# Tuning numbers of a fused decoder block: fewer expert rows on POOL during the key search, more on DVE ahead of the gate spreading, and every eighth instead of every fourth V tile multiplied in plain fp32

## The chip, the core and the metric

The kernel runs on one core of one Trainium2 chip. The metric is device time of one execution in microseconds; before the change three runs gave 1669.54, 1673.44 and 1673.93 us, median 1673.44.

The engines are called as in the profile: PE (matrix multiplication, with PEld for its weight loads), DVE (vector engine), ACT (scalar engine), POOL (GpSimd, which also issues the indirect gathers) and SP (which issues most plain DMAs). Each engine works through its own instructions in a fixed order and waits on semaphores.

## The reference, cut to what matters

One decoder layer on 512 tokens of width 1024: RMSNorm, one input projection, three attention branches, a gated merge, and then a product-key expert layer. All inputs and outputs are fp32. The first half is not touched by the change. The expert layer is:

```python
def peer_ffn(h, w_q, keys1, keys2, u, v):
    q = (h @ w_q).reshape(B, S, PEER_HEADS, 2, half)           # 8 heads
    s1 = einsum('bshd,hkd->bshk', q[..., 0, :], keys1)         # 128 keys each
    s2 = einsum('bshd,hkd->bshk', q[..., 1, :], keys2)
    v1, i1 = top_k(s1, 16); v2, i2 = top_k(s2, 16)
    cand = v1[..., :, None] + v2[..., None, :]
    sv, si = top_k(cand.reshape(..., 256), 16)
    experts = i1[si // 16] * 128 + i2[si % 16]                 # 128 experts per token
    gates = softmax(sv)
    act = gelu(h . u[experts]) * gates
    return sum(act * v[experts])                               # u, v: 16384 x 1024
```

So every token picks 128 of 16384 experts, and needs one row of `u` and one row of `v` for each.

## The kernel before, in words

The 512 tokens are four blocks of 128. The kernel computes the expert layer in two different ways. Blocks 0 and 1 are **gathered**: for each of the 128 choices of a token, POOL issues an indirect DMA that brings one row of `peer_u` or `peer_v` for every one of the 128 tokens (a tile of 128 x 1024 fp32, 512 KB), and an engine consumes it. Such a tile is called a *row* in this document; there are 2 blocks x 2 tables x 128 = 512 rows. Blocks 2 and 3 are **dense**: all 16384 experts are multiplied with the tokens on PE, 128 experts (one *tile* of 512 KB) at a time, first all of `u` (128 U tiles) and then all of `v` (128 V tiles), with a gate that is zero where a token did not choose the expert.

`step()` handles one row. It first issues the gathers of coming rows (line 810), as far ahead as `ahead` allows (AHEAD = 4, or AHEAD + MORE = 6 once the dense part has begun, where two of seven rows take a buffer of another pool), and then consumes the oldest row. A `u` row is one multiply-and-sum on DVE (line 820). A `v` row is normally one multiply-add on DVE (line 829). With `apart=True` it is instead a multiplication on ACT (line 825) and an addition on POOL (line 826). All row additions of a block go into the same tile (`mg` in the profile), so they follow one another.

The rows are spread over the program by counts:

- 176 rows (EARLY_ROWS) run beside the attention of blocks 1 to 3. They are all 128 `u` rows and the first 48 `v` rows of block 0.
- **The search** (`search`, from line 653 on) finds the top keys for blocks 1 to 3. It is a generator that yields a cost for each piece of DVE work; the loop around it adds these costs to a credit, and whenever the credit reaches PER_ROW it does one `step(apart=True)`. The scheduler of the language places these instructions, at low priority. The search also computes the first 8 U tiles (FIRST_U) between its pieces. Its candidate sums (`cand`, line 668) run on POOL, its copies out of PSUM (`qp`, `s`, lines 695 and 702) on ACT.
- From there on DVE, POOL and PE follow the order in which the code is written (`manual_schedule`); ACT and SP are still ordered by the scheduler. PE computes 24 more U tiles (COVER, line 922). Meanwhile DVE does `weigh` (softmax of the gates) and three times `choose` (the experts' numbers, lines 751 to 781), computes a normalised input (`h2n`, line 793), and then BETWEEN rows with `step()`.
- **The spreading** turns the chosen numbers and gates of the dense blocks into dense gates: 64 rounds of one-hot tiles built on DVE (`o`, line 977), scaled on ACT (line 983), multiplied on PE (line 995), with 25 more U tiles and 0.7 rows per round in between. PE cannot start the first round until DVE has built the first `o`, and DVE comes to it only after the BETWEEN rows.
- **The V stage** works through the 128 V tiles, with the last 71 U tiles and all rows that are left spread evenly over it. `fetch_v` (line 1026) issues the load of tile k + 3 on SP while tile k is prepared.

A V tile is multiplied in one of two ways. A **split** tile goes into a `raw` buffer (three of them); ACT casts it to fp32r (`whi`, line 1044), DVE forms the rest (`wlo`, line 126), the same is done for the gated activations (`ah` on ACT, `al` on DVE, line 1046), and PE makes 12 matmuls of 128 x 512 (lines 138 to 140). A **plain** tile, every WHOLE-th, goes into a buffer of its own (`last`, one of it), needs neither ACT nor DVE, and PE makes 4 matmuls in fp32 (line 1060), each of which the profile shows as two records. The `raw` buffer of a split tile is free again once both `whi` and `wlo` have been formed from it.

The loop of the V stage, in which one call prepares tile k + 1 before PE is given tile k:

```python
for k in range(NK):
    now, ready = ready, operands(k + 1) if k + 1 < NK else None
    while done[0] < min(len(JOBS), start + (len(JOBS) - start) * (k + 1) // (NK - 5)):
        step()
    while k_u < min(NK, LAG + (NK - LAG) * (k + 1) // (NK - 10)):
        list(dense_u(k_u))
        k_u += 1
    dense_v(k, *now)
```

Of the kernel before, what the change touches and what calls it, by code (L numbers as in the profile page):

```python
# [29 lines left out]
FIRST_U, COVER, DURING, AFTER = 8, 24, 25, 0  # L30
KEPT = FIRST_U + COVER
SPILT = (128 - KEPT) // 2
BETWEEN, UNWEIGHED, IN_RAW = 12, 14, 0
LAG = FIRST_U + COVER + DURING + AFTER
GA_LATE = 6
URING = 6
# [2 lines left out]
GQ_AT, GQ_PARTS = 1, 4  # L39
RAW_MORE = 5  # L40
STEPS_U = 4
WHOLE, STEPS_N = 4, 0.7
AHD = 3
GSPLIT = 4
GT = 4
# [3 lines left out]
AHEAD, ROWS_IN, MORE = 4, 5, 2  # L49
LATER = 400  # L50
PACE = {"search": 9.0, "choose": 8.0, "rows": 3.5}
EARLY_ROWS, PER_ROW = 176, 2.8


@with_exitstack
# [1168 lines left out]
```

## Time and profile before

The profiled execution took 1678.19 us, of which the span from its first to its last instruction is 1676.2 us; the median of the runs is 1673.44 us, 4.75 us below the profiled one.

| | PE | PEld | DVE | ACT | POOL |
|---|---|---|---|---|---|
| busy, us | 1587.3 | 1371.1 | 1361.5 | 721.4 | 853.2 |
| share of the span | 95% | 82% | 81% | 43% | 51% |

DMA moved 531.79 MB, 317 GB/s on the mean. The mean granted PE clock was 0.977.

How to read it: the profile shows for each instruction its engine, its line in the kernel, its start and its duration, and for the idle time before it the event that ended that idle time. PE's records overlap, since matmuls are pipelined; so the cost of a group of matmuls is read from the start of its first one to the start of the next group, not from the sum of durations. A wait that the profile shows on an engine costs something only if that engine, or one that waits for it, is the one that ends last in that stage.

### The profile page before, as it was taken

To read this page: it belongs to the slowest core of one execution; us is meant where nothing else is said; L and a number is where in the kernel's file an instruction comes from. 1 tells how busy PE (TensorE), PEld (TensorE's weight loads), DVE (VectorE), ACT (ScalarE), POOL (GpSimd) and SP (SyncE) were. 2 spreads that over 40 slices of the span, in tenths; PEclk is the share of its full clock that TensorE was granted. 3 is DMA by queue.
4 is the path that set the end of the run, shared out by engine and by line. 5 is a ranking of instruction groups with operands and counts; after the bars stand their busy time and mean duration, and the time that the engine had idled before them with its cause. 6 is when DMAs were issued, how large, how long until landed. Compare 5 with 4: busy or idle time off the path is not lost.

```text
span 1676.2 us, 25413 instructions
## 1 busy us (share of the span) xinstructions
PE 1587.3 (95%) x8718; PEld 1371.1 (82%) x8718; DVE 1361.5 (81%) x2625; ACT 721.4 (43%) x1586; POOL 853.2 (51%) x664
## 2 busy tenths in 40 slices
PE   6999789999998988998998999999999999999998
PEld 6999679898887988987887999677777777777775
DVE  4777678788988999997998998677777787877886
ACT  6887567546445434543415765222222222222221
POOL 0200251766566455778935544455545555655552
PEclk8999999998998999999999999999999999999999
DMA  6787464898898899767878999999999999999995
GB/s 263 240 262 231 127 199 146 305 354 300 298 344 288 297 338 352 276 212 248 280 247 323 339 354 351 396 405 395 356 389 400 402 397 402 389 401 402 402 368 215
DMA packets 209841, 531.79 MB, mean 317 GB/s; under 512 B 18224, under 2 KB 88112, under 8 KB 209712
## 3 DMA queue, kind: packets, MB, share of 16 engines
q0 software_dynamic: 73728, 268.47, 43.4%
q1 hardware_dynamic: 131376, 249.12, 42.1%
q10 hardware_dynamic: 4608, 12.58, 1.9%
q8 instruction: 69, 1.13, 0.3%
q14 instruction: 60, 0.49, 0.1%
HBM read 515.42 MB, written 14.68 MB: 316 GB/s over the span
## 4 chain that ended last, share of the span: by engine, by line
PE 34%; issue 20%; DMA 20%; POOL 11%; DVE 11%; ACT 2%; SPq 0%; POOLq 0%; DVEq 0%; ACTq 0%
PE mm L922 10%; POOL row L810 9%; DMA row<-in_peer_u_dram,eidx 9%; DMA row<-in_peer_v_dram,eidx 8%; PE mm L139 5%; PE mm L140 5%; PE mm L138 5%; DVE wlo L126 3%; DVE mg L829 2%; DVE scr L820 2%; PE sc L995 2%; PE tp L995 2%; ACT whi L114 1%; POOL mg L826 1%; DMA raw<-in_w_pq_dram 1%
## 5 line engine op out<-in xcount | busy, mean ns | idle before, releaser
L810 POOL DMA_INDIRECT row<-in_peer_u_dram,eidx x256 | 327.0, 1277 | 247.6 <-DVE scr L820 169.4
L810 POOL DMA_INDIRECT row<-in_peer_v_dram,eidx x256 | 331.2, 1294 | 238.1 <-DVE mg L829 170.3
L126 DVE TENSOR_TENSOR wlo<-raw,whi 128x1024 fp32r<-128x1024 f32 (+1 forms) x259 | 327.2, 1265 | 70.0 <-ACT whi L114 41.8
L820 DVE SCALAR_TENSOR_TENSOR scr<-row,h2n 128x1024 bf16<-128x1024 f32 x256 | 313.4, 1224 | 44.3 <-DMA row<-in_peer_u_dram,eidx 42.0
L829 DVE SCALAR_TENSOR_TENSOR mg<-row,acts,mg 128x1024 f32<-128x1024 f32 x222 | 284.7, 1282 | 34.0 <-DMA row<-in_peer_v_dram,eidx 30.7
L114 ACT CAST whi<-raw 128x1024 fp32r<-128x1024 f32 (+1 forms) x172 | 180.5, 1051 | 129.4 <-PE mm L139 59.9
L922 PE MATMUL mm<-h2f,hhi 128*128 128x256 f32 x960 | 220.7, 381 | 2.9 <-ACT ga L924 2.9
L922 PE MATMUL mm<-h2f,hlo 128*128 128x256 f32 x960 | 219.2, 379 | 0.0
L922 PEld LDWEIGHTS mm<-h2f,hlo 128*128 128x128 f32 x960 | 180.5, 190 | 31.9 <-issue 7.2
L922 PEld LDWEIGHTS mm<-h2f,hhi 128*128 128x128 f32 x960 | 180.3, 191 | 27.6 <-ACT ga L924 3.3
L138 PE MATMUL mm<-whi,hhi 128*128 128x256 f32 (+1 forms) x576 | 166.9, 292 | 7.1 <-DVE g L551 1.9
L139 PE MATMUL mm<-wlo,hhi 128*128 128x256 f32 (+1 forms) x576 | 166.1, 289 | 1.0 <-DVE wlo L126 1.0
L140 PE MATMUL mm<-whi,hlo 128*128 128x256 f32 (+1 forms) x576 | 164.3, 287 | 2.4 <-DVE hlo L610 1.6
L924 ACT ACTIVATE ga<-mm 128x256 f32<-128x256 f32 x116 | 44.3, 383 | 279.8 <-PE mm L922 272.1
L1044 ACT CAST whi<-raw 128x1024 fp32r<-128x1024 f32 x96 | 100.3, 1046 | 107.8 <-DMA raw<-in_peer_v_dram 105.7
L138 PE MATMUL mm<-hhi,whi 128*128 128x384 f32 x320 | 111.4, 348 | 7.3 <-ACT ga L924 4.3
L138 PEld LDWEIGHTS mm<-whi,hhi 128*128 128x128 f32 x576 | 109.6, 191 | 10.6 <-ACT hhi L604 2.3
L186 POOL TENSOR_TENSOR rsy<-rsv,mhalf 128x4 f32<-128x4 f32 (+5 forms) x25 | 42.0, 1683 | 145.3 <-DVE rsv L185 144.4
L140 PEld LDWEIGHTS mm<-whi,hlo 128*128 128x128 f32 x576 | 109.8, 191 | 4.5 <-DVE hlo L610 2.0
L139 PEld LDWEIGHTS mm<-wlo,hhi 128*128 128x128 f32 x576 | 110.0, 191 | 3.7 <-DVE wlo L126 1.7
L139 PE MATMUL mm<-hlo,whi 128*128 128x384 f32 x320 | 111.2, 348 | 0.0
L140 PE MATMUL mm<-hhi,wlo 128*128 128x384 f32 x320 | 110.6, 346 | 0.0
(274 smaller groups left out, 3276.4 us busy)
## 6 DMA issues: line engine op xcount, KB each, us to landing
raw<-in_peer_v_dram SPq DMA_DIRECT2D x96, 512.0 KB
hlo<-in_uT_dram SPq DMA_DIRECT2D x60, 512.0 KB
hhi<-in_uT_dram SPq DMA_DIRECT2D x60, 512.0 KB
raw<-in_w_nat_dram SPq DMA_DIRECT2D x40, 512.0 KB
last<-in_peer_v_dram SPq DMA_DIRECT2D x32, 512.0 KB
raw<-in_w_tr_dram SPq DMA_DIRECT2D x48, 256.0 KB
raw<-in_w_o_dram SPq DMA_DIRECT2D x24, 512.0 KB
raw<-in_w_tr_dram SPq DMA_DIRECT2D x24, 512.0 KB
```

Of the source, the lines that this page charges most:

```text
L114: A.copy(hi[:, :n * w], raw[:, :n * w])
L126: V.tensor_sub(lo, raw, hi.bitcast(F32))
L138: PE.matmul(ps, lh, rh, start=first, stop=False)
L139: PE.matmul(ps, lh, rl, start=False, stop=False)
L140: PE.matmul(ps, ll, rh, start=False, stop=last)
L810: G.indirect_dma_start(out=r, out_offset=None, in_=t["peer_" + tab], in_offset=bass.IndirectOffsetOnAxis(ap=eidx[b][:, j:j + 1], axis=0))
L820: V.scalar_tensor_tensor(scr, r, 1.0, h2n[b], op0=OP.mult, op1=OP.mult, accum_out=acts[b][:, c]))
L829: V.scalar_tensor_tensor(x1[b], r, acts[b][:, c], x1[b], op0=OP.mult, op1=OP.add))
L922: PE.matmul(ps[:, :TD], w[:, dc], h2f[dc], start=dc == 0, stop=dc == KC - 1)
L924: A.activation(ga(k), ps[:, :TD], AF.Gelu)
L995: PE.matmul(ps[:, u], o[:, 1, u], o[:, 0, u], start=True, stop=True)
L1044: A.copy(hi, raw)
```

## The change

Three numbers are changed.

```diff
-BETWEEN, UNWEIGHED, IN_RAW = 12, 14, 0
+BETWEEN, UNWEIGHED, IN_RAW = 36, 14, 0
...
-WHOLE, STEPS_N = 4, 0.7
+WHOLE, STEPS_N = 8, 0.7
...
-EARLY_ROWS, PER_ROW = 176, 2.8
+EARLY_ROWS, PER_ROW = 176, 4.6
```

With PER_ROW = 4.6 the search is given 19 rows instead of 34. With BETWEEN = 36 DVE adds 24 more rows ahead of the spreading. The spreading has 44 rows in both, so 237 instead of 246 are left for the V stage. With WHOLE = 8 there are 112 split and 16 plain V tiles, instead of 96 and 32.

On POOL, at the end of the search and after it, the order was this (L826 is an addition of a row, L810 a gather, L668 a candidate sum of the search's last head):

```order
L826 TENSOR_TENSOR mg_2214<-mg_2214,row 128x1024
L668 TENSOR_TENSOR cand<-v_9183 128x3x24
L668 TENSOR_TENSOR cand<-v_9183 128x3x16
L810 DMA row<-in_peer_v_dram,eidx_173 128x1024
L826 TENSOR_TENSOR mg_2214<-mg_2214,row 128x1024
L668 TENSOR_TENSOR cand<-v_9183 128x3x8
L668 TENSOR_TENSOR cand<-v_9183 128x3x16
L810 DMA row<-in_peer_v_dram,eidx_173 128x1024
```

From there gathers and additions alternated until 34 additions were done, and now the same place reads:

```order
L826 TENSOR_TENSOR mg_2214<-mg_2214,row 128x1024
L810 DMA row<-in_peer_v_dram,eidx_173 128x1024
L668 TENSOR_TENSOR cand<-v_9131 128x3x24
L668 TENSOR_TENSOR cand<-v_9131 128x3x16
L668 TENSOR_TENSOR cand<-v_9131 128x3x8
L668 TENSOR_TENSOR cand<-v_9131 128x3x16
L810 DMA row<-in_peer_v_dram,eidx_173 128x1024 x37
```

The first 19 additions stand where they stood, and the 15 that followed, most of them behind the last candidate sum, are gone; on ACT their 15 multiplications (line 825) are gone with them.

On DVE, between the choosing and the first one-hot tile of the spreading (L793 is the normalised input, L829 a row, L977 a one-hot tile, L998 the first product with the gates):

```order
 L793 SCALAR_TENSOR_TENSOR h2n<-mg_7447,rstd,g2r 128x1024
-L829 SCALAR_TENSOR_TENSOR mg_2214<-row,acts_174,mg_2214 128x1024 x12
+L829 SCALAR_TENSOR_TENSOR mg_2214<-row,acts_174,mg_2214 128x1024 x36
 L977 TENSOR_TENSOR o<-tg,eT 128x1024 x4
 L998 TENSOR_TENSOR ga<-sc,ga 128x32x4
```

All four `o` tiles, and so PE's first round, now stand behind 36 rows instead of 12.

On PE, at the fourth V tile, the order was (L922 is a U tile of 8 matmuls, L1060 a plain V tile):

```order
L922 MATMUL mm<-h2f,hhi 128x256 x8
L1060 MATMUL sc<-last,ga 128x512 x2
L1060 MATMUL tp<-last,ga 128x512 x2
L922 MATMUL mm<-h2f,hlo 128x256 x8
L138 MATMUL sc<-whi,ah 128x512
```

and in the place of the plain tile there is now a split one:

```order
L922 MATMUL mm<-h2f,hhi 128x256 x8
L138 MATMUL sc<-whi,ah 128x512
L139 MATMUL sc<-wlo,ah 128x512
L140 MATMUL sc<-whi,al 128x512
L138 MATMUL sc<-whi,ah 128x512
L139 MATMUL sc<-wlo,ah 128x512
```

The U tiles keep their places between the V tiles; 16 of the 32 plain tiles have become twelve matmuls each, with a cast on ACT and two instructions on DVE (lines 126 and 1046) and a `raw` buffer for each.

## The prediction

> **What bounds the kernel now.** The change touches three stretches, so I first asked the table of windows for these: the search of blocks 1 to 3 from its first apart rows to DVE's last instruction of it, the choosing, the rows between, the spreading, the V stage.
>
> ```profile
> 699.50:798.40 98.90, 86.65 (x460) 80.46 (x460) 88.20 (x540) 43.55 (x63) 82.51 (x74) 0.95 0.68 226
> 798.40:869.50 71.10, 68.18 (x317) 59.70 (x316) 66.73 (x94) 21.62 (x35) 46.34 (x27) 1.00 0.78 266
> 869.50:888.60 19.10, 14.72 (x70) 12.72 (x68) 15.33 (x13) 2.35 (x6) 13.59 (x11) 0.97 0.87 319
> 888.60:1039.50 150.90, 149.14 (x931) 138.10 (x932) 142.40 (x186) 103.12 (x350) 71.70 (x60) 0.98 0.94 337
> 1039.50:1672.20 632.70, 624.77 (x2530) 479.16 (x2528) 478.99 (x654) 154.66 (x260) 331.43 (x241) 0.99 1.00 382
> ```
>
> The columns are the stretch and its length, then busy time of PE, PEld, DVE, ACT and POOL, then granted clock, DMA share and GB/s. The V stage is PE's: 624.77 of 632.70 us, with DVE at 479. The spreading is PE's too (149.14 of 150.90). Only from 869.5 to 888.6 does PE have time to spare.
>
> A timeline of PE in the V stage (start, duration, engine, line, operation) says what a tile costs.
>
> ```profile
> 1317.02 1.88 PE L1060 MATMUL sc<-last,late 128*128 128x512 f32 x4
> 1320.45 3.62 PE L922 MATMUL mm<-h2f,hlo 128*128 128x256 f32 x16
> 1323.72 0.58 PE L138 MATMUL sc<-whi,ah 128*128 128x512 f32 x1
> 1326.65 0.40 PE L138 MATMUL sc<-whi,ah 128*128 128x512 f32 x1
> 1329.45 3.62 PE L922 MATMUL mm<-h2f,hlo 128*128 128x256 f32 x16
> 1332.71 0.58 PE L138 MATMUL sc<-whi,ah 128*128 128x512 f32 x1
> ```
>
> From start to start, the plain tile takes 1320.45 - 1317.02 = 3.43 us and the split one that ends at 1329.45 takes 2.80. A U tile takes 3.26, and the split tile behind it, 1323.72 to 1326.65, is longer by 0.13; call it 3.4 together. 96 x 2.80 + 32 x 3.43 + 71 x 3.4 = 620, against the 625 that PE is busy: these prices carry the stage.
>
> **Part 1, every eighth V tile plain.** Sixteen tiles go from 3.43 to 2.80 us on PE: 16 x 0.63 = 10.1 us less. What they add lies on engines that have room only if buffers do. DVE gets 16 forms of `wlo` and `al`, and loses 9 rows:
>
> ```profile
> L126 DVE TENSOR_TENSOR wlo<-raw,whi 128x1024 fp32r<-128x1024 f32 x87 | 106.7, 1226 | 20.8 <-ACT whi L1044 14.7 <-ACT ga L924 4.1 <-issue 2.0
> L1046 DVE TENSOR_TENSOR al<-ga,ah 128x256 fp32r<-128x256 f32 x78 | 32.8, 421 | 53.2 <-ACT ah L1042 53.0
> L829 DVE SCALAR_TENSOR_TENSOR mg<-row,acts,mg 128x1024 f32<-128x1024 f32 x120 | 153.9, 1282 | 25.9 <-DMA row<-in_peer_v_dram,eidx 24.2
> ```
>
> 16 x (1.23 + 0.42) - 9 x 1.28 = +15 us, so 494 of 623 us: 79% busy, from 76%. That is hidden. The 9 rows cost PE nothing and give nothing back.
>
> The buffers are tighter. 96 loads through three `raw` buffers in 633 us left each load 19.8 us; 112 in 623 us leave 16.7. One turn of a buffer, in order of time on SP, ACT, DVE, PE, SP:
>
> ```profile
> 1308.80 0.33 SPq L1026 DMA_DIRECT2D raw<-in_peer_v_dram  x1
> 1317.98 1.05 ACT L1044 CAST whi<-raw 128x1024 fp32r<-128x1024 f32 x1 [0.77 <-DMA raw<-in_peer_v_dram]
> 1327.91 1.22 DVE L126 TENSOR_TENSOR wlo<-raw,whi 128x1024 fp32r<-128x1024 f32 x1
> 1324.84 4.68 SPq L1026 DMA_DIRECT2D raw<-in_peer_v_dram  x2
> ```
>
> The load takes 9.2 us, the cast 1.05, then the data waits 8.9 us for DVE's turn, 1.22 for `wlo`, and the next load (the second of the last row, which ends at 1329.52) goes out at once; PE uses the tile at 1332.71, 3.6 us after `wlo`. So a turn needs 9.2 + 1.05 + 1.22 = 11.5 us and may take 16.7; of the 8.9 us of idling about 3.1 go. That holds on the mean. Where loads are slow it doesn't:
>
> ```profile
> 1409.00 0.37 SPq L1026 DMA_DIRECT2D raw<-in_peer_v_dram  x1
> 1427.48 1.05 ACT L1044 CAST whi<-raw 128x1024 fp32r<-128x1024 f32 x1 [3.30 <-DMA raw<-in_peer_v_dram]
> ```
>
> There 18.5 us passed from issue to cast, a turn of 21. Such stretches, the first tiles, and the last ones, where no U tile gives the loads time, will cost PE something. From below it is nothing (PE has 3.6 us in hand); from above I take one slow turn's excess, 21 - 16.7 = 4.3 us, at three places, 13 us. I take 1.5, near the lower end, since the mean has 5 us of slack a turn. V stage: -10.1 + 1.5 = -8.6 us.
>
> **Part 2, 15 rows fewer on POOL.** The order keeps the first 19 additions where they were, so the search runs as before up to 785. What goes then is a wait. ACT, DVE and PE at the search's end:
>
> ```profile
> 787.14 1.15 ACT L825 ACTIVATE row<-row,acts 128x1024 f32<-128x1024 f32 x1 [7.32 <-DMA row<-in_peer_v_dram,eidx]
> 788.46 0.47 ACT L702 COPY s<-sc 128x384 f32<-128x384 f32 x1
> 788.96 0.68 DVE L657 MAX8 v<-s 128x8 f32<-128x128 f32 x3 [6.79 <-ACT s L702]
> 781.10 0.83 PE L699 MATMUL sc<-keys,qp 128*128 128x128 f32 x6
> 788.61 9.22 PE L922 MATMUL mm<-h2f,raw 128*128 128x256 f32 x32 [3.22 <-ACT ga L924]
> ```
>
> ACT stood 7.32 us before an apart row whose gather had not landed, with the last copy `s` queued behind it, though PE had finished its scores at 781.9; DVE stood 6.79 us for that `s`. This multiplication is one of the 15 that go. `s` can then be copied at 782.0, 6.4 us earlier, and the search ends on DVE at 798.4 - 6.4 = 792.0. PE gains its 3.22, and its U tiles of the cover end near 880.5 instead of 883.7.
>
> The larger effect is in the choosing. DVE's small operations stand still while POOL adds a row:
>
> ```profile
> 802.37 3.63 DVE L736 TENSOR_TENSOR gate<-ex,gden 128x128 f32<-128x128 f32 x3
> 806.08 2.89 DVE L752 TENSOR_SCALAR p<-sh 128x128 f32<-128x128 uint32 x1
> 806.52 2.36 POOL L826 TENSOR_TENSOR mg<-mg,row 128x1024 f32<-128x1024 f32 x1
> 840.73 0.29 DVE L781 TENSOR_TENSOR e<-hot 128x128 f32<-128x128 bf16 x1
> 855.44 0.29 DVE L781 TENSOR_TENSOR e<-hot 128x128 f32<-128x128 bf16 x1
> 855.90 0.23 DVE L752 TENSOR_SCALAR p<-sh 128x128 f32<-128x128 uint32 x1
> 867.51 0.29 DVE L781 TENSOR_TENSOR e<-hot 128x128 f32<-128x128 bf16 x1
> 841.88 2.35 POOL L826 TENSOR_TENSOR mg<-mg,row 128x1024 f32<-128x1024 f32 x1
> ```
>
> The same L752 takes 2.89 us beside an addition (both end at 808.9) and 0.23 after POOL's last one, which began at 841.88. The three choosings end at 840.9, 855.6 and 867.8: 34.9 (from 806.0), 14.7 and 12.2 us. With the 19 additions over by 785 all three take 12.2, which saves 25.2, and the gates ahead of them (the three products of L736 in 3.63 us, which would be near 0.9 at 0.3 each) some 2.7. The stretch of 71.1 us becomes 43, and DVE is ready for rows at 835 instead of 869.5.
>
> **Part 3, 36 rows ahead of the spreading.** This spends what part 2 gave, on the path that sets the end, since PE's first round waits for an `o` that DVE builds behind the rows.
>
> ```profile
> 869.50 10.53 DVE L829 SCALAR_TENSOR_TENSOR mg<-row,acts,mg 128x1024 f32<-128x1024 f32 x8
> 881.25 1.28 DVE L829 SCALAR_TENSOR_TENSOR mg<-row,acts,mg 128x1024 f32<-128x1024 f32 x1 [1.23 <-DMA row<-in_peer_v_dram,eidx]
> 887.40 1.28 DVE L829 SCALAR_TENSOR_TENSOR mg<-row,acts,mg 128x1024 f32<-128x1024 f32 x1 [0.77 <-DMA row<-in_peer_v_dram,eidx]
> 890.36 2.04 PE L995 MATMUL sc<-o 128*128 128x128 f32 x8 [6.14 <-issue]
> 880.00:890.00 10.00, 4.22 (x22) 3.46 (x20) 6.48 (x7) 1.34 (x4) 7.99 (x6) 0.88 1.01 406
> ```
>
> Eight rows that lay ready took 1.32 us each. The next four came 2.05 us apart (881.25 to 887.40 in three steps), held by their gathers, with the DMA at 406 GB/s. From 835: eight rows to 845.6; at 2.05 while PE still draws U tiles, to 880.5, 17 more; the last 11 at 1.32, to 895. The floor is bytes: 29 rows are still to be gathered behind the seven that lie ready, and some 13 U tiles loaded ((880.5 - 835) / 3.4, their six buffers being refilled as they empty), 42 x 0.52 = 22 MB at 406 GB/s, 54 us from 836: 890. I take 893, nearer the paced sum. The spreading starts 893 - 888.6 = 4.4 us later, and PE, done at 880.5, stands 14 us before it. The ends are 882.5 (all 36 at 1.32; then the start is 6 us earlier) and 903 (28 at 2.05; 14 us later).
>
> The Trainium skill (DMA: Bandwidth & Descriptors, section "Where 436 GB/s comes from") puts loads from HBM at about 358 GB/s a core, which speaks against the change: the same bytes would take 61 us, an estimate by that page, the rows would end at 897 and the sum below would be about 4 us worse. The row of 880 to 890 shows 406 GB/s and the V stage 382 over 633 us, so the trace doesn't bear it out, and the sum keeps the measured rate.
>
> The spreading keeps its length; its rounds and its 44 rows are unchanged.
>
> **The sum.** -8.6 + 4.4 = -4.2 us against the profiled 1678.2 us. The profiled execution is 4.8 us above the median of its runs, so I apply the difference to the median: 1673.4 - 4.2 = 1669.2 us. A measurement of this kernel can tell about 0.3%, 5 us, from no change: the three runs shown lie within 4.4.
>
> **The rivals.** First, *the rows keep DVE's pace*. Fewer other loads run from 835 on than I think, or U tiles are fetched well ahead; all 36 rows take 1.32 us, and the spreading starts 6 us earlier, at PE's own end. For it speaks that eight rows in a row did so; against it, the four after them. Sum -8.6 - 6 = -14.6: 1659 us.
>
> Second, *the gathers set the pace throughout*. POOL issues each gather in its own order when a buffer comes free, and these two rows show it at 2.07 us a gather while DVE adds rows:
>
> ```profile
> 885.68 1.77 POOL L810 DMA_INDIRECT row<-in_peer_v_dram,eidx  x1 [0.30 <-issue]
> 887.75 1.76 POOL L810 DMA_INDIRECT row<-in_peer_v_dram,eidx  x1 [0.30 <-issue]
> ```
>
> If that lasts to the end, the spreading starts 14 us later and the sum is -8.6 + 14.4 = +5.8: 1679 us. Against it, 2 us a row is also what a full DMA gives, and its load falls when PE's U tiles are done.
>
> Third, on the slower side too, *the three raw buffers bind in the V stage*. It decides from the point where a turn (load, wait behind SP's other loads, cast, DVE's turn) passes 16.7 us on the mean; then PE waits where it had waited for nothing, and the 10.1 us are given back. At 17.1 us a turn, 112 / 3 x 17.1 = 638 us, the stage is 5.7 us longer than now, and with +4.4 the sum is +10: 1683 us. For it speak the slow loads above; against it, the 8.9 us that a full buffer lay waiting for DVE.
>
> That the change does not do what it says, because the added casts and subtractions on ACT and DVE delay the rows' consumption, falls under the third.
>
> **How the numbers follow.** The forecast, mid stretch 0 to +8 and V stage -10 to -6, a total of -10 to +2, has 0.44: of that 0.16 lies below -5, 0.28 within 5. The first rival has 0.28, all faster. The second has 0.14 and the third 0.14; together 0.02 of them within 5, since they may come in part, and 0.26 slower. So faster 0.44, same 0.30, slower 0.26. The range runs from all gains at once, -10.1 - 6 = -16, 1657 us, to the second rival with the V stage's gain halved, +14.4 - 4.3 = +10, which is also the third: 1684 us; about 0.18 lies outside.
>
> **What would show it.** Right: PE's V stage 8 to 10 us shorter at the same prices a tile, with 16 groups of L1060; DVE's choosing in 43 us with no L752 above 0.3; the search ending near 792; DVE's 36 rows from 835 to about 893 with waits for gathers, and PE idle some 14 us ahead of its first L995. Wrong: waits of PE for `whi` or `wlo` of more than a few us in the V stage, SP waiting for `wlo` ahead of most loads; or rows that end before 885 or after 900.

## The result, and the profile after

The changed kernel takes 1678.85 us (median of 8 runs) against 1669.75 us for the kernel before on the same chip; the ratio is 1.0062, 95% interval [1.0046, 1.0078]. It is slower by 7.7 to 13.0 us; 1669.2 was forecast. The two profiled executions differ by less than the medians, 1682.45 against 1678.19 us, because the one shown of before lay 8.4 us above its median of eight runs and this one 3.6 above. That turns out to matter.

The same stretches in the table of windows of the changed kernel: the search (from its first apart rows), the choosing, the rows up to PE's first product, the spreading, the V stage.

```profile
696.00:788.00 92.00, 79.89 (x438) 75.16 (x436) 87.58 (x540) 38.26 (x58) 73.18 (x68) 0.96 0.67 229
788.00:830.65 42.65, 41.32 (x184) 36.18 (x185) 38.28 (x93) 7.78 (x16) 0.00 (x0) 0.96 0.40 139
830.65:897.42 66.77, 47.19 (x221) 41.32 (x220) 47.91 (x39) 6.34 (x17) 48.80 (x37) 0.88 0.98 389
897.42:1046.74 149.32, 149.32 (x931) 138.19 (x932) 140.29 (x193) 102.58 (x349) 71.89 (x59) 0.99 0.93 333
1046.74:1676.65 629.91, 618.52 (x2594) 491.50 (x2592) 491.88 (x668) 175.87 (x292) 338.20 (x232) 0.99 0.99 377
```

The choosing takes 42.65 us (71.1 before). In the third row PE works 47 of 67 us while the DMA is at 0.98. The V stage is only 2.8 us shorter than the 632.7 before, though PE's busy time in it fell by 6.3. DVE's and ACT's timeline at the search's end and in the choosing:

```profile
778.07 0.48 ACT L702 COPY s<-sc 128x384 f32<-128x384 f32 x1 [0.28 <-issue]
791.97 0.85 DVE L736 TENSOR_TENSOR gate<-ex,gden 128x128 f32<-128x128 f32 x3
792.91 0.23 DVE L752 TENSOR_SCALAR p<-sh 128x128 f32<-128x128 uint32 x1
829.45 1.28 DVE L793 SCALAR_TENSOR_TENSOR h2n<-mg,rstd,g2r 128x1024 f32<-128x1024 f32 x1
830.65 6.56 DVE L829 SCALAR_TENSOR_TENSOR mg<-row,acts,mg 128x1024 f32<-128x1024 f32 x5
838.58 1.28 DVE L829 SCALAR_TENSOR_TENSOR mg<-row,acts,mg 128x1024 f32<-128x1024 f32 x1 [1.38 <-DMA row<-in_peer_v_dram,eidx]
```

The last copy of scores has no apart row ahead of it, the gates' products take 0.85 us (3.63 before) and the first `p` 0.23 (2.89). The rows begin at 830.65. Five of them lie ready; the sixth waits for its gather. How they end, on DVE and PE:

```profile
877.35 0.38 PE L964 MATMUL acc<-cst,e 128*128 128x128 f32 x2
881.45 1.28 DVE L829 SCALAR_TENSOR_TENSOR mg<-row,acts,mg 128x1024 f32<-128x1024 f32 x1 [0.47 <-DMA row<-in_peer_v_dram,eidx]
883.84 11.92 DVE L829 SCALAR_TENSOR_TENSOR mg<-row,acts,mg 128x1024 f32<-128x1024 f32 x9 [1.11 <-DMA row<-in_peer_v_dram,eidx]
895.67 4.61 DVE L977 TENSOR_TENSOR o<-tg,eT 128x1024 f32<-128x1024 f32 x4
897.42 2.04 PE L995 MATMUL sc<-o 128*128 128x128 f32 x8 [19.59 <-issue]
```

PE's work ahead of the spreading ends at 877.8 (its last products start at 877.35); it then stands 19.59 us, until the rest of the rows, the last nine of them in one go, and the first `o` are done. "issue" names no releaser there; the chain is read from DVE's rows and from the order of the code, in which `o` is built on DVE, scaled on ACT and then multiplied on PE. Three windows of that stretch show the DMA full all along, also after PE's last U tile, and PE's clock falling while it idles:

```profile
840.00:850.00 10.00, 10.00 (x48) 8.80 (x47) 5.77 (x5) 0.85 (x3) 7.87 (x7) 1.00 1.02 410
880.00:890.00 10.00, 0.00 (x0) 0.00 (x0) 8.22 (x7) 0.00 (x0) 6.63 (x6) 0.57 1.03 413
890.00:900.00 10.00, 2.58 (x10) 2.52 (x11) 9.86 (x9) 3.08 (x11) 5.08 (x5) 0.50 1.03 413
```

In the V stage the list of waits names PE's (all of them) and the SP queue's (here only those for DVE; SP is the queue that issues the loads of V tiles, line 1026):

```profile
PE sc L138 <- ACT ah L1042: 5.2, 5, 1.6
PE sc L139 <- DVE wlo L126: 2.9, 7, 0.8
PE sc L138 <- ACT whi L1044: 2.8, 2, 1.9
...
SPq L1026 <- DVE al L1046: 136.8, 46, 5.8
SPq L1026 <- DVE wlo L126: 43.3, 16, 4.3
```

PE waits 10.9 us (7.7 before), and 62 waits of SP at its V loads, 180 us in all, end with DVE's `wlo` or `al`, that is, when DVE has just freed a buffer. This is the sign that the third rival (three `raw` buffers bind) would leave. It was one of the first two things to test.

### The profile page after: what moved, and what is told of

Its sections match the earlier page's. It is cut to its first block, busy times and chain, and to the rows that moved or that the text cites. A ratio compares the mean times of both kernels' runs of the same rounds, so it can differ in the third digit from the quotient of the medians.

```text
span 1680.6 us, 25640 instructions
## 1 busy us (share of the span) xinstructions
PE 1578.6 (94%) x8782; PEld 1381.5 (82%) x8782; DVE 1376.6 (82%) x2672; ACT 727.1 (43%) x1603; POOL 837.2 (50%) x649
## 4 chain that ended last, share of the span: by engine, by line
PE 54%; issue 15%; POOL 10%; DMA 10%; DVE 8%; ACT 2%; SPq 0%; POOLq 0%; DVEq 0%; ACTq 0%
PE mm L922 16%; POOL row L810 8%; PE mm L138 7%; PE mm L139 7%; PE mm L140 7%; DMA row<-in_peer_v_dram,eidx 5%; DVE wlo L126 3%; PE sc L995 2%; PE tp L995 2%; DMA raw<-in_peer_v_dram 1%; ACT whi L114 1%; PE sc L140 1%; PE sc L139 1%; PE tp L140 1%; PE tp L138 1%
## 5 line engine op out<-in xcount | busy, mean ns | idle before, releaser
L810 POOL DMA_INDIRECT row<-in_peer_v_dram,eidx x256 | 349.3, 1364 | 264.7 <-DVE mg L829 152.7
L810 POOL DMA_INDIRECT row<-in_peer_u_dram,eidx x256 | 329.4, 1287 | 244.0 <-DVE scr L820 169.0
L126 DVE TENSOR_TENSOR wlo<-raw,whi 128x1024 fp32r<-128x1024 f32 (+1 forms) x275 | 346.1, 1260 | 115.6 <-ACT whi L1044 65.0
L829 DVE SCALAR_TENSOR_TENSOR mg<-row,acts,mg 128x1024 f32<-128x1024 f32 x237 | 303.8, 1282 | 30.3 <-DMA row<-in_peer_v_dram,eidx 27.2
L922 PE MATMUL mm<-h2f,hhi 128*128 128x256 f32 x960 | 220.6, 381 | 0.0
L922 PE MATMUL mm<-h2f,hlo 128*128 128x256 f32 x960 | 219.1, 379 | 0.0
L922 PEld LDWEIGHTS mm<-h2f,hlo 128*128 128x128 f32 x960 | 180.4, 190 | 28.3 <-issue 4.3
L922 PEld LDWEIGHTS mm<-h2f,hhi 128*128 128x128 f32 x960 | 180.4, 191 | 24.5
L1044 ACT CAST whi<-raw 128x1024 fp32r<-128x1024 f32 x112 | 117.0, 1046 | 96.3 <-DMA raw<-in_peer_v_dram 93.0
```

What stands on the lines that cost most here:

```text
L126: V.tensor_sub(lo, raw, hi.bitcast(F32))
L810: G.indirect_dma_start(out=r, out_offset=None, in_=t["peer_" + tab], in_offset=bass.IndirectOffsetOnAxis(ap=eidx[b][:, j:j + 1], axis=0))
L829: V.scalar_tensor_tensor(x1[b], r, acts[b][:, c], x1[b], op0=OP.mult, op1=OP.add))
L922: PE.matmul(ps[:, :TD], w[:, dc], h2f[dc], start=dc == 0, stop=dc == KC - 1)
L1044: A.copy(hi, raw)
```

## The experiments

Three accounts. Theory one: the loss is made ahead of the spreading, behind 36 rows. Theory B (theory two in the first expectations): three buffers eat the V stage's gain. Theory D, formed after the first four runs: the DMA engines are full for nine tenths of the V stage, and a faster PE only waits more often. "First copy of scores" is ACT's first L702 of the three blocks' search; the change touches no code ahead of it, and yet it came anywhere from 670.4 to 681.9 us in these executions. So the middle is measured from it. The length of a V stage is always that of one profiled execution, a time that of the median.

### Only the V tiles

```diff
-WHOLE, STEPS_N = 4, 0.7
+WHOLE, STEPS_N = 8, 0.7
```

> Only WHOLE = 8 (16 plain V tiles instead of 32); search, choosing and the 12 rows as before. Theory one (the loss is made ahead of the spreading, where PE now idles 19.6 us behind 36 rows): the V stage alone still gains, by the 2.8 us that the two profiled executions differ or up to the 8.6 us forecast, so 1661 to 1667 us against a median of 1669.75. Theory two (the three raw buffers take the gain and more, and the loss of about 9 us is made in the V stage): 1672 us or more, with PE waiting for whi, wlo and ah for over 10 us in that stage.

1663.36 us, ratio 0.9982 [0.9962, 1.0001]: about 3 us, at the edge of what can be told. The V stage took 631.27 us, hardly less than before, with PE busy for 618.12. So the V tiles are not where the time was lost, nor do they bring what was forecast. PE waited 12.4 us for `whi`, `wlo` and `ah` in that stage, which is theory two's sign, but no loss came of it. This kernel runs before's program up to the V stage, and here that looks different: PE's first product came at 875.20, 203.7 us behind the first copy of scores at 671.50, with PE idle for 2.86 us. In the execution shown of before it was 890.36 - 679.92 = 210.4 us and 6.14.

### Only the rows

```diff
-BETWEEN, UNWEIGHED, IN_RAW = 12, 14, 0
+BETWEEN, UNWEIGHED, IN_RAW = 36, 14, 0
-EARLY_ROWS, PER_ROW = 176, 2.8
+EARLY_ROWS, PER_ROW = 176, 4.6
```

> Only the rows (PER_ROW = 4.6 and BETWEEN = 36), every fourth V tile plain as before. Theory one: PE's first round of the spreading starts 7 us later than before (897 against 890), after some 20 us of idling, and nothing gives it back: 1676 to 1680 us, V stage within 2 us of its 632.7. Theory two: the middle costs less than 4 us: 1670 to 1674 us.

1680.49 us, ratio 1.0085 [1.0063, 1.0108]. On PE, and on ACT for the first copy of scores:

```profile
674.68 0.50 ACT L702 COPY s<-sc 128x384 f32<-128x384 f32 x1
897.43 2.04 PE L995 MATMUL sc<-o 128*128 128x128 f32 x8 [20.50 <-issue]
```

That is 222.8 us behind the scores, and the V stage took 630.95 us, no longer than before. The whole loss is here; theory one holds.

### The same with 12 and with 24 rows

Both have PER_ROW = 4.6 and every fourth V tile plain; the second has BETWEEN = 24 as well.

```diff
-EARLY_ROWS, PER_ROW = 176, 2.8
+EARLY_ROWS, PER_ROW = 176, 4.6
```

> Only PER_ROW = 4.6, with 12 rows ahead of the spreading as before; the 15 rows that POOL no longer adds all go to the V stage (261 instead of 246). Theory one: rows end near 848, so the first round comes as soon as PE's cover ends, at 878 instead of 890: 1657 to 1660 us if the V stage carries 15 more rows at no cost. Rival (the V stage is held by its DMA, whose share is 1.00 there): 15 more rows of 0.52 MB at 382 GB/s are 20 us more, so 1672 to 1678 us.

> PER_ROW = 4.6 with 24 rows ahead of the spreading, every fourth V tile plain; 249 rows for the V stage (246 before). Seven ready rows from 831 and 17 at 2.05 us end at 875, before PE's cover does at 878. Theory one: the first round starts at 878 to 880, 10 to 12 us earlier than before, V stage as before: 1658 to 1660 us. Rival (the DMA's backlog of U tiles and rows only moves, and the spreading or the V stage gives the time back): 1666 us or more.

With 24 rows PE's first product comes when PE's own cover is done, as theory one says:

```profile
673.01 0.49 ACT L702 COPY s<-sc 128x384 f32<-128x384 f32 x1
870.48 0.38 PE L964 MATMUL acc<-cst,e 128*128 128x128 f32 x2
873.32 1.32 PE L995 MATMUL sc<-o 128*128 128x128 f32 x8 [2.35 <-issue]
```

200.3 us behind the scores, 21 earlier than with 36 rows. But the time is 1668.95 us, ratio 1.0017 [0.9992, 1.0043]; with 12 rows it is 1697.39, ratio 1.0192 [1.0168, 1.0216], although there too PE starts on time (877.06). Their rivals had the direction: the V stage takes back what the middle gives. For 12 rows it takes back far more than the rival's 1672 to 1678 us. Its windows, with 249 and 261 rows left to it:

```profile
1020.68:1656.11 635.43, 625.78 (x2530) 478.95 (x2528) 482.86 (x660) 155.57 (x260) 328.84 (x244) 0.99 1.00 383
```

```profile
1024.42:1691.06 666.64, 635.61 (x2530) 482.11 (x2528) 498.32 (x679) 156.05 (x260) 339.65 (x256) 0.98 0.98 375
```

Most of PE's waits in the second of them come through `ah`, which ACT makes from gates that DVE multiplies in its turn behind the rows:

```profile
PE sc L138 <- ACT ah L1042: 24.0, 13, 5.1
```

PE works on the same tiles as before in both, and yet 15 rows more than before's 246 made the stage 34 to 37 us longer. From this comes theory D, with two windows of the changed kernel, one from the stage's middle and its last 70 us:

```profile
1397.00:1467.00 70.00, 69.98 (x299) 55.96 (x297) 54.99 (x64) 18.39 (x31) 39.63 (x27) 1.00 1.03 393
1607.00:1677.00 70.00, 65.77 (x258) 47.92 (x256) 56.10 (x69) 18.62 (x30) 28.33 (x19) 1.00 0.77 281
```

In stretches of 63 us the DMA's share is 0.95 to 1.04 from the stage's start to some 63 us before its end, and 0.73 in the last; only there is it free.

### Four buffers

```diff
-            pool, n = (gp[0], 1) if k % WHOLE == WHOLE - 1 else (wp, None)
+            pool, n = (gp[0], 1) if k % 4 == 3 else (wp, None)
```

So every fourth tile, split or plain, goes into the buffer `last`. The first run is the changed kernel with this edit, the second the kernel before with WHOLE = 8 and this edit.

> The changed kernel, but every fourth V tile still goes into the buffer of its own (last) that it had before, split or plain; so the split tiles have four buffers as in the kernel before, and PE's order is that of the changed kernel. V stage of the changed kernel 629.9 us. Theory B (three raw buffers take the gain): the stage falls to 622 to 625 us, PE's waits in it from 11 to under 6 us, and the time to 1671 to 1674 us. Theory D (the DMA engines are full for nine tenths of that stage, and PE, made faster, only waits for them more often): stage 628 to 632 us, time 1676 to 1682 us.

> The kernel before with WHOLE = 8 and the same four buffers; rows as before (246 in the V stage). Theory B: V stage 623 to 626 us against 631.3 with three buffers, and 1656 to 1660 us against 1663.4. Theory D: 629 to 633 us in the V stage, 1662 to 1667 us.

The changed kernel with four buffers: 1684.89 us, ratio to before 1.0108 [1.0071, 1.0145], above what either theory expected. The execution profiled was the quickest of its five, 1674.53 us. Its V stage and PE's waits in it:

```profile
1039.52:1668.73 629.21, 614.28 (x2594) 490.31 (x2592) 491.81 (x668) 175.83 (x292) 326.40 (x232) 0.99 0.99 377
```

```profile
PE sc L138 <- ACT ah L1042: 14.3, 7, 5.7
PE sc L139 <- DVE wlo L126: 0.2, 1, 0.2
```

629.21 against 629.91 us, and PE waits 14.5 us instead of 10.9: the waits for `whi` and `wlo` went, those for `ah` grew. The other kernel took 1669.17 us, ratio 1.0019 [1.0002, 1.0036], slower than with three buffers (0.9982), with 637.74 us in the V stage; that too is more than either theory expected. So the fourth buffer does not bring the gain that theory B promised. It does not make SP's waits go either: 151 of the 180 us for `wlo` and `al` are left in the changed kernel. What those waits are worth is shown by the next run, which keeps them. Why the fourth buffer costs time is not shown; a load let out earlier that only shares a full DMA with the gathers would do it.

### Sixty rows, and before once more

```diff
-BETWEEN, UNWEIGHED, IN_RAW = 36, 14, 0
+BETWEEN, UNWEIGHED, IN_RAW = 60, 14, 0
```

> The changed kernel with 60 rows ahead of the spreading, so 213 instead of 237 in the V stage; asked for the length of that stage alone. The spreading starts 24 x 1.3 to 24 x 2.05 us later (31 to 49). Theory D: the V stage moves 24 x 0.52 = 12.6 MB less, its DMA share falls to about 0.95, and it takes 618 to 623 us. Theory B: 628 to 632 us still, since the V tiles have the same three buffers. Time 1700 to 1730 us either way.

> The kernel before, unchanged, for a second profiled execution of it. If the one that the forecast was made from is typical, PE stands some 6 us ahead of its first product of the spreading, which comes 210 us behind the first copy of scores (s) of the three blocks' search. If it was a late one, as the execution with only the V tiles changed suggests (203.7 us, PE idle for 2.9), it comes near 204 us, and the span is near 1666.

With 60 rows the time is 1704.07 us (one run), since the spreading starts at 930.80. But the V stage, with 213 rows, the same three buffers and the same tiles:

```profile
1080.25:1698.30 618.05, 613.16 (x2594) 489.08 (x2592) 461.90 (x620) 174.69 (x292) 293.64 (x208) 1.00 0.97 363
```

Here is the gain that was forecast: 11.9 us less than the changed kernel's, with PE idle for 4.9 us in all. SP waits 181 us for `wlo` and `al` here too, so this wait in full view held nothing. Theory D holds against B.

Before's second execution took 1666.49 us. ACT and PE in it:

```profile
677.27 0.50 ACT L702 COPY s<-sc 128x384 f32<-128x384 f32 x1
876.06 0.38 PE L964 MATMUL acc<-cst,e 128*128 128x128 f32 x2
882.36 2.04 PE L995 MATMUL sc<-o 128*128 128x128 f32 x8 [5.82 <-issue]
```

Its V stage in the table of windows:

```profile
1031.14:1660.50 629.36, 622.76 (x2530) 478.21 (x2528) 479.11 (x654) 155.18 (x260) 323.08 (x241) 1.00 1.00 384
```

The first product comes 205.1 us behind the scores: the one shown first was a late one, as supposed, though the 5.82 us of idling is like it. And the V stage of the same program differs by 3.3 us between two executions.

### Half of the V tiles, half of the U tiles

Both start from the changed kernel and leave out half of a table's bytes. The diffs show the loads alone; the other lines let the engines use the loaded half twice, in instructions of the same sizes.

```diff
-            nc.sync.dma_start(v_raw[k], t["peer_v"][k * NK:(k + 1) * NK])
+            nc.sync.dma_start(v_raw[k][:, :512], t["peer_v"][k * NK:(k + 1) * NK, :512])
```

> The changed kernel, but of each V tile only its first 512 columns are loaded (256 KB instead of 512) and used for both halves; so it leaves out half of the V table. PE, ACT, DVE and POOL do the same instructions on tiles of the same size, the 237 rows and the three buffers stay. Only the DMA's bytes fall in the V stage, by 128 x 0.26 = 34 MB. Theory D (the DMA's bytes hold the rows, these hold DVE, and DVE holds PE): V stage 613 to 620 us instead of 629.9, DVE's waits for rows under 5 us. Rival E (a row's own cost on POOL and DVE, or the three buffers, holds it): 627 to 632 us. The stretch from the first copy of scores to the first product of the spreading stays at 219 to 223 us.

```diff
-        nc.sync.dma_start(u_raw[k], t["uT"][k])
+        nc.sync.dma_start(u_raw[k][:, :512], t["uT"][k][:, :512])
```

> The changed kernel, but of each U tile from the ninth on only its first half is loaded (256 KB) and its four chunks are used twice; so it leaves out half of those U tiles' weights. All instructions on PE, DVE and POOL stay. If the DMA's bytes pace the 36 rows (U tiles and gathers together filled it at 410 to 413 GB/s from 840 to 900 us), the rows now run near DVE's 1.32 us: 36 in 48 to 53 us instead of 64.7, and the first product of the spreading comes 204 to 210 us behind the first copy of scores instead of 221. If POOL's issue of a gather paces them (1.75 + 0.30 us each in that stretch), it stays at 219 to 223. The V stage loads 71 x 0.26 = 18.6 MB less as well: 614 to 620 us by theory D, 627 to 632 by theory E. Time 1648 to 1658 us by the first of each, 1676 to 1682 by the second.

The V stages of the two, with 237 rows and three buffers each, one run each:

```profile
1047.22:1663.89 616.67, 610.54 (x2594) 490.12 (x2592) 491.74 (x668) 178.36 (x292) 324.94 (x232) 1.00 0.92 331
```

```profile
1042.91:1664.64 621.73, 614.88 (x2594) 492.39 (x2592) 492.21 (x668) 175.72 (x292) 324.65 (x232) 0.99 0.96 354
```

All engines do the same work; only bytes are missing, and the stage falls from 629.91 to 616.67 and 621.73 us, more than the 3.3 us by which it differed between two executions of before. Theory E (a row's own cost on POOL and DVE) falls; it is the bytes. The times were 1669.69 and 1670.46 us, the second some 12 us above what I had expected of it. There the first product came 213.4 us behind the scores, between the 204 to 210 expected and the 221 of the changed kernel: the rows ahead of the spreading ran faster, but not at DVE's pace. The two windows, from the first row to the first `o`, of the changed kernel and of half U:

```profile
830.65:895.67 65.02, 47.19 (x221) 41.29 (x219) 46.16 (x37) 5.84 (x15) 47.91 (x37) 0.89 0.98 388
```

```profile
834.72:891.77 57.05, 42.97 (x201) 37.59 (x199) 46.17 (x37) 5.45 (x14) 43.66 (x37) 0.91 0.96 369
```

25.2 MB in 65.0 us and 21.1 MB in 57.1: 4.2 MB less, 8 us less. Bytes pace these rows too, and not a fixed price of a gather on POOL: the same 37 gathers kept it busy for 43.66 us instead of 47.91. (What sets a single gather's time there, 0.94 to 1.97 us in this stretch, no run tells.) That they would reach DVE's 1.32 us was my mistake: the DMA stayed at 407 to 411 GB/s from 850 to 890, filled now by the gathers.

### Later ends, and the best version

The first run is the kernel before with WHOLE = 8 and this edit, the second the changed kernel with BETWEEN = 24 and this edit: rows and U tiles are spread further towards the end of the V stage, where the DMA is free.

```diff
-        while done[0] < min(len(JOBS), start + (len(JOBS) - start) * (k + 1) // (NK - 5)):
+        while done[0] < min(len(JOBS), start + (len(JOBS) - start) * (k + 1) // (NK - 2)):
             step()
-        while k_u < min(NK, LAG + (NK - LAG) * (k + 1) // (NK - 10)):
+        while k_u < min(NK, LAG + (NK - LAG) * (k + 1) // (NK - 5)):
```

> The kernel before with WHOLE = 8, three buffers, and the rows of the V stage spread over it up to its last tile but two (before: but five), its U tiles up to the last but five (before: but ten); so the DMA's full stretch carries some 2.5% less at a time and the last 70 us, at a share of 0.80 now, more. Theory D: V stage 626 to 629 us against 631.3 with the ends as they were, and 1659 to 1663 us, faster than both kernels by 0.3 to 0.5% of the one before. Theory E, or if the last U tiles and rows now hold PE at the end: 631 to 636 us in the stage, 1663 to 1670 us.

> All of the change but with 24 rows ahead of the spreading instead of 36 (249 in the V stage), and the late ends. The first product of the spreading comes at PE's own end, about 200 us behind the first copy of scores instead of 221. Theory D: with 249 rows and PE faster the V stage is held by the DMA, 632 to 637 us; 1660 to 1667 us, 12 to 18 us faster than the changed kernel and within 0.4% of the one before. If the late ends take the DMA's excess away: 626 to 630 us in the stage and 1656 to 1660 us.

The first: 1666.49 us, ratio 0.9993 [0.9974, 1.0012], no difference, though its V stage was 626.50 us in the execution profiled; 1659 to 1663 had been expected. The second: 1663.82 us, ratio 0.9970 [0.9949, 0.9991], and 0.9% under the changed kernel by the two ratios to before, 0.9970 and 1.0062. Its first product came at 875.53, 200.3 us behind the scores; its V stage:

```profile
1024.56:1657.45 632.89, 618.67 (x2594) 489.54 (x2592) 505.75 (x692) 176.57 (x292) 339.15 (x244) 0.99 1.00 384
```

It is the only version here whose interval lies below the kernel before, by little: PE's middle is repaired, the V stage still held by its bytes.

## Why the prediction was wrong

**Part 2 was right.** The order, the waits and the prices came as worked out: the choosing in 43 us, rows from 830.65 (835, less the 3.5 us that this execution was earlier at the first copy of scores), no `p` above 0.23, PE's cover ending at 877.4 (880.5 less 3.5, 877.0, was forecast).

**The middle, +4.4, is the step that failed most: +14.8 on the mean.** Measured from the first copy of scores, the first product came 221.0 us behind it here, and at 222.8, 219.2 and 222.8 in the other three with 36 rows (only the rows, four buffers, half V). In the five executions that have before's middle it came at 210.4, 205.1, 203.7, 204.8 and 209.3: mean 206.7. Two errors of like sign make the 10 us between +4.4 and +14.8:

1. The base. I read the start of the spreading, 888.6, from one execution, knew that it lay 4.8 us above its median, and took that excess to lie anywhere. 3.7 us of it lay in this very stretch (210.4 against 206.7), so the forecast credited the change with the removal of waits that a usual execution has less of. DVE's wait for the last `s` is one: 6.79 us in that execution, 5.2 to 6.1 in the other four. The rest of the 3.7 is not traced.
2. The rows. 58 us were forecast, 65.0 came. Eight rows were priced as lying ready, since eight did before; five did. So 22 rows and not 17 went at the gathers' pace, at 2.12 us each, and nine and not 11 at 1.32 behind them. The paced sum said 60 and I had shaded it to 58 by a count of bytes, 22 MB. That count took 29 gathers; but POOL refills each buffer for the rows behind the 36 as well, and SP loaded 15 U tiles from 829 on, not 13. 25.2 MB went through. The pace of 2 us a row did not end with PE's last U tile at 877 but lasted until 883.84.

The rate of 406 GB/s was right from 840 on: 410 to 413 until 900, with 236 in the ten us before, where the gathers had only begun again. The Trainium skill (DMA: Bandwidth & Descriptors, section "Where 436 GB/s comes from") has about 358 as a core's limit to HBM, half of a stack's 716; the estimate by that page, 61 us for the rows, lay nearer than mine. By the trace that was luck: there were more bytes, and the rate while the DMA was full was above the page's.

**The V stage, -8.6, came to -1.1** (629.9 against 632.7 and 629.4 in two executions of before, mean 631.0). The price of a tile held. Gelu of the same two U tiles, eighteen apart, in a stretch without stalls, before and after:

```profile
1123.57 0.39 ACT L924 ACTIVATE ga<-mm 128x256 f32<-128x256 f32 x1 [5.76 <-PE mm L922]
1273.63 0.38 ACT L924 ACTIVATE ga<-mm 128x256 f32<-128x256 f32 x1 [2.99 <-PE mm L922]
```

```profile
1132.65 0.39 ACT L924 ACTIVATE ga<-mm 128x256 f32<-128x256 f32 x1 [5.73 <-PE mm L922]
1280.13 0.39 ACT L924 ACTIVATE ga<-mm 128x256 f32<-128x256 f32 x1 [2.87 <-PE mm L922]
```

150.06 and 147.48 us: 2.58 us over some 3.7 exchanged tiles, 0.69 each (0.63 was forecast). What failed is the +1.5 for stalls, the second term that was mis-sized, and its reason. I asked whether a buffer's turn fits, found 5 us of slack, and passed over the last two columns of my own first table: DMA share 1.00, 382 GB/s in that stage. A stall in the changed kernel, on ACT and PE, and the window behind it:

```profile
1303.12 1.04 ACT L1044 CAST whi<-raw 128x1024 fp32r<-128x1024 f32 x1 [6.43 <-DMA raw<-in_peer_v_dram]
1308.29 1.04 ACT L1044 CAST whi<-raw 128x1024 fp32r<-128x1024 f32 x1 [3.82 <-DMA raw<-in_peer_v_dram]
1309.96 0.50 PE L138 MATMUL sc<-whi,ah 128*128 128x512 f32 x1 [1.57 <-ACT ah L1042]
```

```profile
1310.00:1315.00 5.00, 4.82 (x13) 3.49 (x14) 4.96 (x9) 2.27 (x3) 2.58 (x3) 0.66 1.03 418
```

Two V tiles come late. DVE stands 4.3 us behind the first; `ah`, for which PE waits 1.6 us, stands on ACT behind the second. PE then runs at a granted clock of 0.66 for the next 5 us. Over the stage PE was idle for 11.4 us, against 7.9 and 6.6 in the two executions of before, and a lowered clock (what the granted clock lacks to 1, summed over windows of 5 us) took 5.1 us against 3.4 and 1.7. Together that is 5 to 8 us of the 10.1 given back; some 2 us more are not accounted for. With 60 rows the two were 4.9 and 1.7 us.

**The rivals.** The second (gathers set the pace throughout) comes nearest, for the middle: 65 us against its 68. That its 1679 us is the measured median is luck in part: it added 5.8 us to 1673.4, and 7.7 to 13.0 came on top of 1669.75. The third was right that the V stage gives its gain back through waits, and wrong in the cause and in the 5.7 us by which it was to become longer. The first did not occur.

**The sum.** +14.8 - 1.1 = +13.7, and the spreading, 149.3 against 149.1 and 148.8, adds 0.4; the medians say +7.7 to +13.0. The difference is within what these stages scatter by from one execution to the next. The medians of the two halves fit better: the rows alone cost 14.2 us (1.0085), the V tiles alone gave 3.0 (0.9982), which makes +11.

Left open: why 12 rows more than 249 cost the V stage 31 us, when their 6.3 MB would take 16 at 400 GB/s. PE was idle for 31.0 us there against 9.7, and the stage's mean rate fell from 383 to 375 GB/s, so it was not the bytes alone. No run tells whether late gathers that block one another do that.

## What to carry to other kernels

Before pricing a stage by its busiest engine, look at the DMA share in the same row: a stage that shows PE at 99% and the DMA at 1.00 has two bounds, and most of the time saved on the one can be lost to the other. Work that is moved takes its bytes with it, and the place to put it is where the DMA idles (0.40 in the choosing), not ahead of an engine that waits. And take the base of a difference from more than one execution, or measure it from a nearby event that the change does not touch.

## What the runs showed of the hardware

- Plain loads and indirect gathers together ran at 410 to 413 GB/s for 60 us, and the V stage at 375 to 386 GB/s over its 626 to 667 us, in the eleven profiled executions that moved all bytes and had at most 36 rows ahead of the spreading.
- Code ahead of the change came 670.4 to 681.9 us into fourteen executions: 11 us of scatter before anything differed.
- PE's granted clock fell to 0.57 and 0.50 in the 20 us in which it idled. The spreading behind it was hardly longer than before's, ahead of which PE idled 6 us (149.3 against 148.8 and 149.1 us). In six executions with 2.4 to 3.5 us of idling it took 147.4 (three) and 149.0 (three).
